# Attention queries of a two-layer hybrid encoder: evicted with 64 partitions at a time, or with 128 and copies to their places

## Chip, cores and metric

The kernel runs on one NeuronCore of one Trainium2 chip. The metric is device time in microseconds (us), the median over runs of the same program; lower is better. The profile comes from one execution taken by the hardware profiler.

## What is computed

One inference step of a small encoder trunk with two layers for 1024 prompt frames and 32 sample frames (1056 columns in all), model width 1024, all in fp32. Layer 0 is an mLSTM mixer and a SwiGLU feed-forward; layer 1 is windowed attention with 16 query heads on 2 shared key/value heads of width 64, and a second feed-forward. Each sub-layer ends in `x = LayerNorm(alpha * x + sublayer(x))`. The part that matters here:

```python
q = (x @ w_q).reshape(B, nc, CHUNK, N_KV_HEADS, GROUP, HEAD_DIM)
s = einsum('bcqhgd,bckhd->bchgqk', q, k) * (HEAD_DIM ** -0.5) + bias
mx = maximum(max(s, -1), sink)
p = exp(s - mx)
p = p / (sum(p, -1) + exp(sink - mx))
o = einsum('bchgqk,bckhd->bcqhgd', p, v)
```

Frames see their own chunk of 64 and the two chunks before it, with an ALiBi bias and a learned sink per head.

## The kernel before

**Precision.** Each fp32 operand of a large product is split into a rounded high part and a low part (the rest), both of type fp32r. `gemm` (L352) makes each product from three matmuls: high times high (L360), high times low (L361), low times high (L362). ScalarE rounds the high part and VectorE or GpSimd subtracts it to get the low part; for weights this is `Weights._next` (L182, the cast at L200 and the subtraction at L202). Raw weights come in by DMAs on SyncE's queue (`load_to`, L159) into three buffers, and a load is issued as soon as the second half of the unit three before it has been split, so it waits for the subtraction that read that buffer.

**Order.** Instructions are emitted in program order, engine by engine, and each engine and SyncE's queue run them in that order. `Weave` (L69) interleaves tasks: after each step of a `gemm` (three matmuls) it advances a clock by an estimate of the step's time, and every task (a generator) whose pause is over emits its next piece. So a task's `yield 2.0` means "go on after 2.0 us of projection have been emitted". Where the program must wait for a task without a projection to emit, it ticks the clock by 0.25 with nothing in between.

**Attention** (layer 1). The 1056 columns lie in three groups g of 384, 384 and 288 (`GRP`). Pairs of query heads are numbered j = 0 to 7. `q_group(j, g)` (L1574) projects one pair for one column group (8 steps of `gemm`) into a PSUM bank `d`, and makes the tile `Q` of shape [128, 2, 384]: for the first head of the pair (index 0) the high part on partitions 0 to 63 and the low part on 64 to 127; for the second head (index 1) the high part on 64 to 127 and the low part on 0 to 63. The key tiles `KH` and `KL` carry the keys twice along the partitions, so one matmul over 128 partitions multiplies high and low parts of a query at once. Before the change ScalarE writes the two high parts (L1580, L1581), 64 partitions each, and VectorE the two low parts (L1582, L1585), across to the other half of the partitions. There are four buffers of `Q`, so a group is projected only after the scores of the group four before it are emitted (L1785).

The queries come in the order `QG` (L1758): the four (j, 0) of j = 0 to 3 are projected first (L1627), then keys and values of the other columns, then the remaining 20 groups while attention runs. `attention` (L1650) is a pipeline over blocks (j, b) of 128 queries, three blocks to a group: `scores` (four matmuls L1669, L1670 into the two banks `psS`, which VectorE empties with bias and row minimum, L1675), `soft` (exponentials on ScalarE, L1687; reciprocal on VectorE, L1691; scaling on GpSimd, L1693), `turn` (transposes by TensorE into the one bank `T`, L1713; high part by ScalarE, L1716; low part by VectorE, L1717), `values` (L1728, L1729) and `place` (L1737, L1739). The scores of a group are emitted only when `ast["ready"]` says that its queries are made; the task `q_made` (L1777) raises it 2.0 us of emitted projection after the group's projection.

SyncE's queue carries, besides the weights, the copies that spread the keys over both partition halves (`k_spread`, L1547 to L1551, 96 KB each for a group of 384 columns), the bias tiles (L1607, L1608), and late in attention the reloads of the residual (L1098, L1100). `mixed_parts` (with L390 and L391) splits the attention output for the next projection while attention still runs.

Of the kernel before, what the change touches and what calls it, by code (L numbers as in the profile page):

```python
# [9 lines left out]
F32 = mybir.dt.float32  # L10
F32R = mybir.dt.float32r
AF = mybir.ActivationFunctionType
ALU = mybir.AluOpType
# [3 lines left out]
P = 128  # L17
# [223 lines left out]
def kernel(ctx: ExitStack, tc: tile.TileContext, A, O):  # L241
    nc = tc.nc
    ctx.enter_context(tc.manual_schedule())
    wv = Weave()
# [3 lines left out]
    def pool(name, space=None, side=None):  # L248
        kw = {}
        if space is not None:  # L250
            kw["space"] = space
        if side is not None:
            kw["side"] = side
        return tc.tile_pool(name=name, bufs=1, reuse_waits="tile", **kw)

    def new(p, tag, shape, dt=F32, bufs=1):
        uid[0] += 1
        return p.tile(list(shape), dt, name=f"{tag}_{uid[0]}", tag=tag, bufs=bufs)
# [124 lines left out]
    def project(u, g):  # L383

        ps = psdense(g)
        gemm(ps, wcols(u), xcols(g))
        return ps
# [1138 lines left out]
    pb = eb.enter_context(pool("pb"))  # L1526
# [47 lines left out]
    def q_group(j, g):  # L1574

        t0, n = GRP[g]
        ps = project(U_QB[g > 0][j], g)
        q = Q[j, g] = new(pb, "Q", [P, 2, 384], F32R, bufs=4)
        sc = -(HD ** -0.5)
        nc.scalar.activation(q[0:64, 0, :n], ps[0:64], AF.Copy, scale=sc)  # L1580
        nc.scalar.activation(q[64:128, 1, :n], ps[64:128], AF.Copy, scale=sc)  # L1581
        nc.vector.scalar_tensor_tensor(  # L1582
            q[64:128, 0, :n], ps[0:64], sc, q[0:64, 0, :n].bitcast(F32), op0=ALU.mult, op1=ALU.subtract
        )
        nc.vector.scalar_tensor_tensor(  # L1585
            q[0:64, 1, :n], ps[64:128], sc, q[64:128, 1, :n].bitcast(F32), op0=ALU.mult, op1=ALU.subtract
        )

    ck = new(pb, "ck", [P, P])
    nc.sync.dma_start(ck[:], A["cache_k"])  # L1590
# [4 lines left out]
    def v_parts(c, src, L):  # L1595

        src = src.rearrange("p (g d) -> p g d", g=2)
        nc.scalar.copy(VR[:L, c, :, 0, :], src)
        nc.vector.tensor_sub(VR[:L, c, :, 1, :], src, VR[:L, c, :, 0, :].bitcast(F32))
# [25 lines left out]
        wv.drain(t)  # L1625
    keys_values(0)
    for j in range(4):  # L1627
        q_group(j, 0)
        W.done(U_QB[0][j])
    for t in tasks[2:]:  # L1630
        wv.drain(t)
# [7 lines left out]
    def v_turn(group, pause):  # L1639
        yield pause  # L1640
        for c, c0, L, g, off in CH:
            if g == group:
                pt = new(psb, "O", [P, 512], bufs=2)
                nc.tensor.transpose(pt[:L, :P], vT[g][:, off : off + L], ident[:])
                v_parts(c, pt[:L, :P], L)
                ast["v"] = c + 1
                yield 0.8
# [112 lines left out]
    visits = [*range(4), *range(8)]  # L1760
    for t in spread:
        wv.drain(t)
    wv.launch(v_turn(0, 0))
    task = wv.launch(attention((GAP_A,) * 8))
    ast["ready"] = 4
# [9 lines left out]
    nc.sync.dma_start(O["s_v"], vT[2][:, 256:])  # L1775

    def q_made():  # L1777
        yield 2.0
        ast["ready"] += 1

    for i, (j, g) in enumerate(QG):
        if i < 4:
            continue

        while ast["scored"] < 3 * (i - 3):  # L1785
            wv.tick(0.25)
        q_group(j, g)
        wv.launch(q_made())
        if g == 2:
            W.done(U_QB[1][j])  # L1790
        if (j, g) == (7, 0):
            nparts[0] = 0
            parts = wv.launch(
                mixed_parts(
                    scr,
                    lambda g: ast["ready"] > QG.index((7, g)),
                    lambda k, g: ast["placed"] >= 3 * QG.index((k, g)) + 3,
                    (1.6, 1.0, 1.0),
                )
            )  # L1800
# [145 lines left out]
```

## Time and profile before

| | |
|---|---|
| median of 3 runs | 2269.16 us (2268.02 to 2269.37) |
| the profiled execution | 2261.86 us, span 2259.8 us, mean granted TensorE clock 0.996 |
| first and last query eviction in the span | 1212.2 us and 1413.6 us |
| ScalarE query instructions (L1580, L1581) | 24 each, median 480 and 486 ns |
| VectorE query instructions (L1582, L1585) | 24 each, median 550 and 559 ns |
| SyncE's queue (q1) | 284.38 MB, 37.1% of the DMA engines' time |
| DMA, mean over the span | 129 GB/s |

How to read it: times in the profile are us from the start of the span, durations of single instructions are ns or us as marked. PE is TensorE's matmul, PEld its weight load, DVE is VectorE, ACT ScalarE, POOL GpSimd, SP SyncE. A group of rows names the line, engine, operation, `out<-in`, shapes (partitions x elements) and count. "idle before, releaser" is the time that an engine stood still ahead of an instruction and what ended it.

### The profile page before, as it was taken

The page shows a single profiled execution, that of the slowest core. Times are in us where ns is not written, and L with a number is a line of the kernel's source. Part 1 is how long each engine was busy: PE and PEld are TensorE (multiplying, and loading weights), DVE is VectorE, ACT ScalarE, POOL GpSimd, SP SyncE. Part 2 cuts the span into 40 slices and gives each one's busy share as a digit, 9 for nine tenths or more (in the row PEclk, how much of TensorE's full clock was granted, in tenths as well). Part 3 has the DMA queues.
Part 4 walks back from the last instruction along what each step waited for, and adds up shares of the span by engine and source line. Part 5 has one row for each costly group of instructions (what it writes and reads, how often), then busy time and mean ns, then how long its engine had stood idle before and what let it go on. Part 6 is the DMA issues. An engine that isn't in the chain of part 4 may idle for free. (4 is left out here: it accounts for less than half of the span.)

```text
span 2259.8 us, 44187 instructions
## 1 busy us (share of the span) xinstructions
PE 2189.0 (97%) x17086; PEld 2149.0 (95%) x17086; DVE 1490.3 (66%) x2807; ACT 1015.3 (45%) x2285; POOL 1135.6 (50%) x1042
## 2 busy tenths in 40 slices
PE   9999999998999999999998999999999999999997
PEld 9899999998999999999997998899899999999997
DVE  4465577778666665566667778877666666466657
ACT  4443354455444444322246778756444444421124
POOL 2544333226666666544326776633666666554422
PEclk9999999999999999999999999999999999999999
DMA  4222112211434443697424211421343344397712
GB/s 148 74 54 69 53 39 85 96 39 66 150 137 153 158 143 139 219 333 234 162 79 138 85 60 44 137 72 47 115 152 140 135 146 163 124 334 259 248 57 77
DMA packets 167393, 291.52 MB, mean 129 GB/s; under 512 B 16592, under 2 KB 123144, under 8 KB 167184
## 3 DMA queue, kind: packets, MB, share of 16 engines
q1 hardware_dynamic: 162832, 284.38, 37.1%
q10 hardware_dynamic: 4352, 4.33, 0.5%
q8 instruction: 134, 2.20, 0.4%
q14 instruction: 75, 0.61, 0.1%
HBM read 203.89 MB, written 82.94 MB: 127 GB/s over the span
## 5 line engine op out<-in xcount | busy, mean ns | idle before, releaser
L202 POOL TENSOR_TENSOR wl_s<-wr,wh_s 128x512 fp32r<-128x512 f32 x224 | 316.8, 1435 | 241.3 <-ACT wh_s L200 158.2
L360 PE MATMUL d<-sx,wh 128*128 128x264 f32 (+2 forms) x1068 | 340.2, 319 | 1.2 <-DVE act L1505 0.7
L362 PE MATMUL d<-sx,wl 128*128 128x264 f32 (+2 forms) x1068 | 325.6, 305 | 8.4 <-DVE wl L202 6.0
L361 PE MATMUL d<-sx,wh 128*128 128x264 f32 (+2 forms) x1068 | 324.6, 304 | 3.8 <-DVE sx L474 2.6
L200 ACT CAST wh_s<-wr 128x512 fp32r<-128x512 f32 x224 | 135.5, 617 | 316.6 <-DVE wr L177 289.2
L360 PE MATMUL A<-sx,wh_s 128*128 128x264 f32 x896 | 254.6, 284 | 3.3 <-ACT z L1338 3.3
L202 POOL TENSOR_TENSOR wl<-wr,wh 128x512 fp32r<-128x512 f32 (+2 forms) x103 | 141.4, 1379 | 231.7 <-ACT wh L200 200.6
L361 PE MATMUL A<-sx,wh_s 128*128 128x264 f32 x896 | 254.2, 284 | 0.0
L362 PE MATMUL A<-sx,wl_s 128*128 128x264 f32 x896 | 254.0, 283 | 0.0
L362 PEld LDWEIGHTS d<-sx,wl 128*128 128x128 f32 x1068 | 200.9, 188 | 10.8 <-DVE wl L202 7.6
L361 PEld LDWEIGHTS d<-sx,wh 128*128 128x128 f32 x1068 | 201.6, 189 | 5.8 <-DVE sx L474 3.1
L360 PEld LDWEIGHTS d<-sx,wh 128*128 128x128 f32 x1068 | 201.7, 189 | 5.1 <-ACT z L443 1.1
L202 POOL TENSOR_TENSOR wl_a<-wr,wh_a 128x512 fp32r<-128x512 f32 x112 | 169.4, 1520 | 49.0 <-ACT wh_a L200 42.2
L362 PE MATMUL d<-sx,ex 128*128 128x264 f32 x624 | 178.5, 286 | 5.0 <-DVE ex L202 4.9
L360 PE MATMUL d<-sx,ex 128*128 128x264 f32 x624 | 181.0, 290 | 0.8 <-ACT sx L390 0.8
L361 PE MATMUL d<-sx,ex 128*128 128x264 f32 x624 | 178.2, 286 | 1.8 <-DVE sx L391 1.7
L360 PEld LDWEIGHTS A<-sx,wh_s 128*128 128x128 f32 x896 | 168.4, 188 | 3.7 <-ACT z L1338 3.7
L362 PEld LDWEIGHTS A<-sx,wl_s 128*128 128x128 f32 x896 | 168.9, 188 | 0.0
L361 PEld LDWEIGHTS A<-sx,wh_s 128*128 128x128 f32 x896 | 168.4, 188 | 0.0
L1208 POOL TENSOR_TENSOR z<-z 128x528 fp32r<-128x528 f32 x76 | 105.2, 1384 | 105.0 <-issue 53.2
L1693 POOL TENSOR_SCALAR s<-s,st 128x256 f32<-128x256 f32 (+1 forms) x144 | 124.2, 874 | 55.7 <-DVE st L1691 46.4
L1207 ACT CAST z<-z 128x528 fp32r<-128x528 f32 x136 | 85.8, 631 | 97.8 <-DVE z L1220 47.7
(334 smaller groups left out, 7404.2 us busy)
## 6 DMA issues: line engine op xcount, KB each, us to landing
wr<-in_gu SPq DMA_DIRECT2D x96, 512.0 KB, 4.5
hs_x<-z SPq DMA_DIRECT2D x72, 528.0 KB, 2.8
hs_t<-z SPq DMA_DIRECT2D x64, 528.0 KB, 4.1
sx<-hs_x SPq DMA_DIRECT2D x112, 264.0 KB, 6.0
sx<-hs_t SPq DMA_DIRECT2D x64, 264.0 KB, 6.0
ex<-hs_t SPq DMA_DIRECT2D x64, 264.0 KB, 6.2
wr<-in_dn SPq DMA_DIRECT2D x32, 512.0 KB, 5.2
ex<-hs_x SPq DMA_DIRECT2D x32, 264.0 KB, 6.1
```

Of the source, the lines that this page charges most:

```text
L200: self.nc.scalar.copy(hi, r)
L202: eng.tensor_sub(lo, r, hi.bitcast(F32))
L360: nc.tensor.matmul(out, ah, bh, start=start and k == 0, stop=False, **kw)
L361: nc.tensor.matmul(out, ah, bl, start=False, stop=False, **kw)
L362: nc.tensor.matmul(out, al, bh, start=False, stop=stop and k == last, **kw)
L1207: nc.scalar.copy(hi.bitcast(F32R), buf(s))
L1208: eng.tensor_sub(lo.bitcast(F32R), buf(s), hi)
L1693: nc.gpsimd.tensor_scalar_mul(p[:R, h, lo:256], p[:R, h, lo:256], st[:R, 2, h : h + 1])
```

## The change

`q_group` now writes the high parts of both heads with one ScalarE instruction of 128 partitions into a tile `qh`, and the low parts with one VectorE instruction of 128 partitions into a tile `ql` (two buffers each, 128 x 384). A task `place`, launched by `q_group`, waits for 1.0 us of emitted projection and then issues four DMAs on SyncE's queue that copy 64 partitions each to the four places in `Q`. The task that raises `ast["ready"]` waits for 4.0 us in place of 2.0. Ahead of the start of attention the last of the first four placements is emitted at the latest. The matmuls are the same in number and shape; their order in attention follows from the tasks.

```diff
@@ q_group
         q = Q[j, g] = new(pb, "Q", [P, 2, 384], F32R, bufs=4)
+        h, l = (new(pb, tag, [P, 384], F32R, bufs=2)[:, :n] for tag in ("qh", "ql"))
         sc = -(HD ** -0.5)
-        nc.scalar.activation(q[0:64, 0, :n], ps[0:64], AF.Copy, scale=sc)
-        nc.scalar.activation(q[64:128, 1, :n], ps[64:128], AF.Copy, scale=sc)
-        nc.vector.scalar_tensor_tensor(
-            q[64:128, 0, :n], ps[0:64], sc, q[0:64, 0, :n].bitcast(F32), op0=ALU.mult, op1=ALU.subtract
-        )
-        nc.vector.scalar_tensor_tensor(
-            q[0:64, 1, :n], ps[64:128], sc, q[64:128, 1, :n].bitcast(F32), op0=ALU.mult, op1=ALU.subtract
-        )
+        nc.scalar.activation(h, ps, AF.Copy, scale=sc)
+        nc.vector.scalar_tensor_tensor(l, ps, sc, h.bitcast(F32), op0=ALU.mult, op1=ALU.subtract)
+
+        def place():
+            yield 1.0
+            for i in range(2):
+                own, other = slice(64 * i, 64 * i + 64), slice(64 - 64 * i, 128 - 64 * i)
+                nc.sync.dma_start(q[own, i, :n].bitcast(F32), h[own].bitcast(F32))
+                nc.sync.dma_start(q[other, i, :n].bitcast(F32), l[own].bitcast(F32))
+
+        return wv.launch(place())
@@ the first four groups
-        q_group(j, 0)
+        placing = q_group(j, 0)
@@ ahead of attention
     for t in spread:
         wv.drain(t)
+    wv.drain(placing)
     wv.launch(v_turn(0, 0))
@@ q_made
-        yield 2.0
+        yield 4.0
         ast["ready"] += 1
```

## The prediction

> **What bounds the kernel now.** I read the page's engine shares first, then a table by stage of the stretch in which queries are made and used, then the waits of TensorE there, then single rows in order of time.
>
> ```profile
> span 2259.8 us, 44187 instructions
> ...
> PE 2189.0 (97%) x17086; PEld 2149.0 (95%) x17086; DVE 1490.3 (66%) x2807; ACT 1015.3 (45%) x2285; POOL 1135.6 (50%) x1042
> ```
>
> TensorE is busy for 97% of the span, so an edit to ScalarE and VectorE work pays only where TensorE waits for it. The stages (columns: stretch, length, then busy us of PE, PEld, DVE, ACT, POOL, then granted clock, DMA share, GB/s):
>
> ```profile
> 1210.00:1240.00 30.00, 22.24 (x125) 20.91 (x125) 22.89 (x50) 21.77 (x54) 20.72 (x19) 0.89 0.50 159
> 1240.00:1300.00 60.00, 58.27 (x429) 56.43 (x429) 46.38 (x174) 45.24 (x140) 43.82 (x57) 1.00 0.28 80
> 1300.00:1370.00 70.00, 69.59 (x507) 66.77 (x506) 56.65 (x215) 56.30 (x174) 51.73 (x65) 1.00 0.15 49
> 1370.00:1420.00 50.00, 44.38 (x329) 41.73 (x328) 45.01 (x155) 42.24 (x127) 30.48 (x36) 1.00 0.26 76
> ```
>
> The reader is to see two places with TensorE idle: 7.8 us in 1210 to 1240, where attention begins, and 5.6 us in 1370 to 1420, where VectorE is busy 90% and ScalarE 84%. From 1300 to 1370 TensorE has 0.4 us idle, and cheaper evictions buy nothing there. The waits of TensorE in 1200 to 1450 (total, times, longest):
>
> ```profile
> PE psS L1669 <- DVE st L1675: 6.6, 2, 5.6
> PE T L1713 <- DVE lo L1717: 5.2, 4, 2.3
> ```
>
> One wait of 5.6 us for VectorE to empty the score banks, and four for VectorE to empty the bank of the transposed probabilities. These are what can shrink.
>
> **The change part by part.** *Evictions.* 24 query groups each take two ScalarE and two VectorE instructions of 64 partitions:
>
> ```profile
> L1580 ACT ACTIVATE Q<-d x24: 386/480/488, 1212.2 to 1413.6; 64x384 fp32r<-64x384 f32 x16, 64x288 fp32r<-64x288 f32 x8
> L1581 ACT ACTIVATE Q<-d x24: 406/486/488, 1212.7 to 1414.0; 64x384 fp32r<-64x384 f32 x16, 64x288 fp32r<-64x288 f32 x8
> L1582 DVE SCALAR_TENSOR_TENSOR Q<-d,Q x24: 450/550/552, 1215.2 to 1415.1; 64x384 fp32r<-64x384 f32 x16, 64x288 fp32r<-64x288 f32 x8
> L1585 DVE SCALAR_TENSOR_TENSOR Q<-d,Q x24: 459/559/561, 1215.7 to 1415.5; 64x384 fp32r<-64x384 f32 x16, 64x288 fp32r<-64x288 f32 x8
> L1572 DVE COPY act<-d x3: 447/547/550, 1210.8 to 1263.5; 128x384 f32<-128x384 f32 x2, 128x288 f32<-128x288 f32 x1
> ```
>
> The last row reads the same kind of bank with all 128 partitions in 0.55 us, the time of the 64-partition forms. So one instruction does the work of two: about 0.48 us of ScalarE and 0.56 us of VectorE go per group, 11.5 and 13.4 us in all. Which of this lies on the path is a question of the place.
>
> *First scores.* After its first four score products TensorE waits for this chain:
>
> ```profile
> 1229.33 0.48 ACT L1580 ACTIVATE Q<-d 64x384 fp32r<-64x384 f32 x1
> 1229.83 0.49 ACT L1581 ACTIVATE Q<-d 64x384 fp32r<-64x384 f32 x1
> ...
> 1230.34 0.55 DVE L1582 SCALAR_TENSOR_TENSOR Q<-d,Q 64x384 fp32r<-64x384 f32 x1 [0.56 <-ACT Q L1581]
> 1230.91 0.56 DVE L1585 SCALAR_TENSOR_TENSOR Q<-d,Q 64x384 fp32r<-64x384 f32 x1
> 1231.50 0.29 DVE L1599 TENSOR_TENSOR VR<-O,VR 128x128 fp32r<-128x128 f32 x1
> 1231.71 0.28 DVE L1675 CUSTOM_DVE_ANT_0 s<-psS,bt 128x129 f32<-128x129 f32 x1
> ...
> 1232.05 0.58 PE L1669 MATMUL psS<-KH,Q 128*128 128x256 f32 x1 [5.61 <-DVE st L1675]
> ```
>
> In this order one ScalarE instruction (0.49) and one VectorE instruction (0.56) leave the chain. The group before it loses the same pair, but there the engines also waited for others. I take -1.2 us, a little over the 1.05 of one group; the ends are 0 (the value split, L1599, then waits for something else) and -2.1 (both groups in full). The two stretches around this wait ran at half clock:
>
> ```profile
> 1228.40:1231.80 3.40, 0.00 (x0) 0.00 (x0) 2.80 (x5) 2.76 (x6) 3.40 (x3) 0.50 0.76 194
> 1231.80:1235.20 3.40, 3.15 (x13) 3.06 (x14) 1.54 (x10) 1.59 (x8) 3.02 (x6) 0.50 0.30 106
> ```
>
> The 3.15 us of products in the second row would take half at full clock, so up to 1.6 us hang on whether the shorter wait still trips the clock; an earlier restart into the same slow stretch costs up to 0.6 more. I take 0. The Trainium skill, TensorE: Matmul & The Clock Gate, section "Part 1: The HAM clock gate", says that the clock halves after an idle window of some 3.4 us in a free-running grid; by it a wait cut from 5.6 to 4.4 us would contain a whole window less often, and the sum would be lower by up to 1.6 us. The rows agree on the 3.4 us, but the drop came while only the stretch before, partly busy, was over, so I do not count on it.
>
> *The copies.* Four SyncE copies of 96 KB per group, 96 in all. The nearest rows are the copies of the keys, between partition halves with the same shape:
>
> ```profile
> L1548 SPq DMA_DIRECT2D KH<-KH x4: 594/596/605, 1205.8 to 1262.7; - x4
> ...
> DMA to landing us min/median/max: 2.2/2.2/2.2
> ...
> DMA to landing us min/median/max: 3.6/3.9/4.2
> ...
> DMA to landing us min/median/max: 2.0/2.0/2.0
> ```
>
> (The landings are of L1548, L1547 and L1551.) Four issues of 0.6 take 2.4 us of SyncE, and a copy lands 2.0 to 4.2 us after its issue: a query is whole some 4 to 6 us after its low part, less the 1 us that the shorter evictions give. Attention needs the first group after the restart soonest:
>
> ```profile
> 1269.26 0.36 SPq L159 DMA_DIRECT2D wr<-in_wqb  x1
> ...
> 1270.11 0.56 DVE L1585 SCALAR_TENSOR_TENSOR Q<-d,Q 64x384 fp32r<-64x384 f32 x1
> ...
> 1271.20 0.28 PE L1669 MATMUL psS<-KH,Q 128*128 128x256 f32 x1
> ```
>
> Scores come 0.5 us after the query is done, so unmoved they would stall by 3 to 4 us. The longer delay of q_made moves them: in the emitted order the scores of this group now stand five projection steps later (one of 288 and four of 384 columns, some 2.5 us). SyncE is free at 1269.7, issues until about 1272, and the last copy lands at 1273.4 to 1275.6; the moved scores are due at 1273.8. So 0 to 1.8 us, and I take 0.2, as the last copy of a run is like the 2.0 rows. Later groups have room; the last one is evicted at 1413.60 and scored 25 us later:
>
> ```profile
> 1413.60 0.40 ACT L1580 ACTIVATE Q<-d 64x288 fp32r<-64x288 f32 x1
> ...
> 1438.64 0.28 PE L1669 MATMUL psS<-KH,Q 128*128 128x256 f32 x1
> ```
>
> *Lost cover.* Projection is fixed in amount, and attention starts 2.5 us later beside it. What runs alone at the restart is missing later: in the emitted order the attention steps that follow each other without a projection step between go from 11 to 18. What one costs, from both ends:
>
> ```profile
> 1345.11 0.28 PE L1729 MATMUL O<-lo,VR 128*128 128x256 f32 x1
> 1345.22 0.28 PE L1669 MATMUL psS<-KH,Q 128*128 128x256 f32 x1
> ...
> 1407.75 0.63 PE L1713 MATMUL T<-ident,s 128*128 128x128 f32 x4 [2.34 <-DVE lo L1717]
> ```
>
> Values and next scores back to back at 1345 cost nothing (0.11 apart, the pace). Three such places in a row at 1404 cost 2.3 us. Of the new ones five are single, and one cluster of three lies near the 36th block. I take 1.5 us for all; the ends are 0 and 6 (0.9 each).
>
> *The late stage.* The 2.3 us wait itself hung on VectorE:
>
> ```profile
> 1404.62 0.45 DVE L1582 SCALAR_TENSOR_TENSOR Q<-d,Q 64x288 fp32r<-64x288 f32 x1
> 1405.09 0.46 DVE L1585 SCALAR_TENSOR_TENSOR Q<-d,Q 64x288 fp32r<-64x288 f32 x1
> ...
> 1406.91 0.69 DVE L1717 TENSOR_TENSOR lo<-T,hi 128x512 fp32r<-128x512 f32 x1
> ```
>
> Six groups are evicted from 1370 to 1420, so up to 3.4 us of VectorE time go in a stage with 5.6 us of idle TensorE. The order is the same there before and after. I take half, -1.7; the ends are 0 (waits for GpSimd and ScalarE step in) and -5.6 (all the idle time, if the 0.48 on ScalarE counts as well).
>
> **Sum**: -1.2 + 0 + 0.2 + 1.5 - 1.7 = -1.2 us. The profiled execution took 2261.86 us (span 2259.8 and 2.06 around it), so 2260.7 for one like it. The median of the runs shown is 2269.16, 7.3 above, so 2268.0.
>
> **The rivals.**
> *SyncE's order (slower).* The copies stand in one queue with the weight loads, and these wait for buffers:
>
> ```profile
> SPq L159 <- POOL wl L202: 94.3, 12, 19.9
> ```
>
> Twelve waits, 7.9 us in the mean. A query behind one lands 7.9 + 2.4 + 2.2 = 12.5 us after its low part. In the first three groups after the restart the room is 0.5 to 4 us now and some 3 to 7 after the move: one such case stalls TensorE by 6 to 9 us, and the sum becomes +5 to +8, 2275. It decides where a load in front of a query is issued over 3 us after the query's low part is made. For it: the second group after the restart stands behind such a load. Against: at 1269 the load went out before the query was done. Chance 0.27, with dearer lost cover counted in, which leads to the same side at 6 us without relief.
> *VectorE was the bound (faster).* If the late stage runs at the pace of VectorE and ScalarE, all of the 5.6 us go, and with the first scores -6.8, and up to 1.6 of the clock: 2261 to 2262.4. For it: 90% busy, and the longest wait there behind VectorE. Against: no wait there names a query eviction itself. Chance 0.28.
> *The change does not do what it says*: 128 partitions cost twice 64. Then nothing is relieved and the sum is +1.7, 2270.9. The L1572 row speaks against it; 0.02, inside the forecast's band.
> By the Trainium skill, DMA: Bandwidth & Descriptors, section "Rules for kernel authors", two transfers to disjoint partition halves serialise and one of 128 partitions is better; by it the last copy of four lands late, as in the 3.6 to 4.2 rows, which makes 1.8 of the 0.2 above and the sum +0.4.
>
> **How the numbers follow.** The forecast, within 0.2% (4.5 us, about what a measurement of this kernel can tell from no change), has 0.45 with the third rival; faster 0.28; slower 0.27. The range reaches from the fast rival's 2262 to the slow one's 2275.
>
> **What would show it.** Right: query evictions x24 on each engine at 0.48 and 0.55 us; the 5.6 us wait near 4.4; scores of the fifth group some 2.5 us later against its projection without a long wait; TensorE idle in 1370 to 1420 down by about 2 us. Wrong: a wait of scores or weights for a copy of several us, SyncE waiting with copies behind a load, half clock at a second place, or new waits of the transposes between 1300 and 1370 that add up to over 4 us.

## The result, and the profile after

The changed kernel takes 2263.38 us (median of 20 runs, 2258.93 to 2268.05), the kernel before, run beside it, 2267.94 us (20 runs, 2263.73 to 2272.42). The ratio is 0.9983, 95% interval 0.9977 to 0.9990: 2.3 to 5.2 us faster. That is inside the band of 0.2% that was forecast, at its fast edge, where the sum had said 1.2 us.

The two profiled executions must not be subtracted. That of before took 2261.86 us, 6 us under the median of its runs; that of after took 2266.14 us, 3 us over its own. The mean granted clocks say which way each was lucky (one row from the view of the cores for before, then for after):

```profile
core 0: 2259.8 us, clock 0.996
```

```profile
core 0: 2263.9 us, clock 0.992
```

What can be compared is each stage. From the page of after, the engine shares, against the row shown of before: VectorE is 15.7 us and ScalarE 11.5 us less busy.

```profile
PE 2197.0 (97%) x17086; PEld 2157.3 (95%) x17086; DVE 1474.6 (65%) x2783; ACT 1003.8 (44%) x2261; POOL 1136.1 (50%) x1042
```

The rows of the two eviction lines and of the copies in after (count, minimum/median/maximum in ns, first and last start):

```profile
L1581 ACT ACTIVATE qh<-d x24: 395/482/498, 1213.9 to 1414.4; 128x384 fp32r<-128x384 f32 x16, 128x288 fp32r<-128x288 f32 x8
```

```profile
L1582 DVE SCALAR_TENSOR_TENSOR ql<-d,qh x24: 445/547/559, 1216.8 to 1415.4; 128x384 fp32r<-128x384 f32 x16, 128x288 fp32r<-128x288 f32 x8
```

```profile
L1588 SPq DMA_DIRECT2D Q<-qh x48: 461/505/618, 1218.4 to 1418.1; - x48
...
DMA to landing us min/median/max: 2.0/2.3/4.7
```

Half as many instructions of the same length, and 96 copies (48 of this line, 48 of L1589) with an issue of about half a microsecond. The view could tell the landing of only a few of them. The table by stage of after (columns as before: stretch, length, busy us of PE, PEld, DVE, ACT, POOL, granted clock, DMA share, GB/s):

```profile
1210.00:1240.00 30.00, 24.83 (x136) 22.68 (x135) 20.23 (x44) 18.59 (x45) 22.36 (x22) 0.94 0.78 220
1240.00:1300.00 60.00, 56.58 (x402) 54.83 (x403) 39.91 (x154) 40.12 (x127) 39.32 (x51) 0.97 0.40 108
...
1370.00:1420.00 50.00, 47.08 (x358) 45.41 (x357) 42.93 (x162) 41.92 (x130) 34.77 (x43) 1.00 0.40 114
```

Against before, TensorE's busy time goes up by 2.6 us in the first row and 2.7 us in the last (1370 to 1420), and down by 1.7 us in the second. The waits of TensorE in after, 1200 to 1450 (total, times, longest):

```profile
PE psS L1673 <- DVE st L1679: 4.0, 2, 3.1
PE T L1717 <- DVE st L1695: 2.8, 3, 1.5
PE T L1717 <- DVE lo L1721: 2.6, 4, 1.0
PE psS L1673 <- DMA Q<-qh: 1.4, 1, 1.4
...
PE psS L1673 <- DMA Q<-ql: 0.3, 1, 0.3
```

The wait of the first scores fell from 5.6 to 3.1 us, those of the transposes for their low part from 5.2 to 2.6, while those for the reciprocal (`st`) rose from 2.1 to 2.8; and one new wait of 1.4 + 0.3 us stands for the copies at the restart. A fourth place is outside the stages that I had looked at: in 1450 to 1500, where attention runs out, after has a wait for a split of the next weights that before has not. The waits of TensorE there, before and then after:

```profile
PE d L362 <- DVE ex L202: 2.0, 1, 2.0
...
```

```profile
PE d L362 <- DVE ex L202: 2.2, 1, 2.2
...
PE d L362 <- POOL ex L202: 1.2, 1, 1.2
PE ln L421 <- DVE z L602: 0.4, 1, 0.4
```

**A ledger by matmul number.** All kernels here issue the same 17086 matmuls. So I lined up two profiles by the number of the matmul. A stretch at half clock (granted 0.50) slows the work that falls into it, whichever that is; so I took from each time half of TensorE's busy time in the stretches at half clock up to there, and read how many us each stage is longer than in the first profile of before (minus is faster). Stages by number, with their times in before: first scores 9100 to 9250 (1206 to 1241 us), restart 9450 to 9550 (1270 to 1284), middle 9550 to 10200 (to 1373), late stage 10200 to 10500 (to 1420), end of attention 10500 to 11000 (to 1488). "Half clock" is what was taken off over the whole span, in us.

| profile | first scores | restart | middle | late | end | half clock |
|---|---|---|---|---|---|---|
| before, second profile (e9) | -0.7 | 0.0 | 0.0 | 0.0 | -0.1 | 11.0 (first: 3.2) |
| after | -2.1 | +1.7 | -0.5 | -3.9 | +1.9 | 13.4 |
| e1 change without the delay | -1.7 | +6.3 | -1.1 | -3.9 | +0.5 | 9.9 |
| e2 delay alone | 0.0 | 0.0 | +2.6 | +1.1 | +1.7 | 14.9 |
| e3 relief alone | -3.6 | 0.0 | -1.1 | -3.9 | -0.4 | 11.8 |
| e4 first three groups direct | -2.8 | 0.0 | +0.2 | -4.2 | -0.2 | 8.5 |
| e5 change in the first four groups | -3.0 | 0.0 | 0.0 | 0.0 | +0.4 | 10.2 |
| e6 change in the last twelve | +1.0 | 0.0 | -0.2 | -4.1 | +0.3 | 15.8 |
| e7 relief, copies nobody reads | -1.1 | 0.0 | -1.0 | -3.9 | -0.4 | 9.4 |
| e8 change at both ends | -2.5 | 0.0 | 0.0 | -4.1 | -0.1 | 14.3 |
| e10 halves, no crossing | 0.0 | 0.0 | 0.0 | -0.4 | -0.7 | 11.5 |
| e11 first copies from ScalarE | -2.6 | +0.2 | -0.4 | -3.9 | +1.5 | 13.8 |
| e12 relief and delay | -3.7 | 0.0 | -0.5 | -3.7 | +1.3 | 9.5 |

How far to trust it: where nothing was altered, the first column reads between -0.7 (e9) and +1.0 (e6), and the kernels whose first four groups are evicted alike spread from -1.1 to -3.7 in it, so it is good to about 1.3 us. Restart and middle repeat to 0.2, the late stage to 0.4 and the end to 0.7 (e10). In the four kernels with the delay in every group the matmuls from 9459 to 10229 stand in another order, which counts up to 0.4 us of the middle's work to the restart. Ahead of 9100 and behind 11000, where no kernel differs, the ledger still moves by -1.4 to +2.0 and -2.6 to +0.6 us; so it tells stages, not totals.

### The profile page after: what moved, and what is told of

Same layout as the page of the kernel before. It is cut to its first block, busy times and chain, and to the rows that moved or that the text cites. A ratio compares the mean times of both kernels' runs of the same rounds, so it can differ in the third digit from the quotient of the medians.

```text
span 2263.9 us, 44340 instructions
## 1 busy us (share of the span) xinstructions
PE 2197.0 (97%) x17086; PEld 2157.3 (95%) x17086; DVE 1474.6 (65%) x2783; ACT 1003.8 (44%) x2261; POOL 1136.1 (50%) x1042
## 4 chain that ended last, share of the span: by engine, by line
PE 79%; DVE 8%; ACT 4%; DMA 3%; issue 3%; POOL 2%; SPq 1%; ACTq 0%; DVEq 0%; POOLq 0%
PE A L360 9%; PE A L362 9%; PE A L361 9%; PE d L360 9%; PE d L362 9%; PE d L361 8%; PE B L360 7%; PE B L361 7%; PE B L362 7%; PE T L1717 1%; DMA wr<-in_dn 1%; PE T L904 1%; DMA hs_t<-z 1%; PE psS L1673 1%; PE H L900 1%
## 5 line engine op out<-in xcount | busy, mean ns | idle before, releaser
L361 PEld LDWEIGHTS d<-sx,wh 128*128 128x128 f32 x1068 | 204.3, 191 | 5.7 <-DVE sx L474 3.0
L360 PEld LDWEIGHTS d<-sx,wh 128*128 128x128 f32 x1068 | 204.3, 191 | 4.9 <-ACT z L443 1.1
L360 PE MATMUL A<-ex,wh_s 128*128 128x264 f32 x448 | 127.7, 285 | 1.3 <-ACT z L1321 1.3
```

The lines of the kernel that those rows point to most:

```text
L360: nc.tensor.matmul(out, ah, bh, start=start and k == 0, stop=False, **kw)
L361: nc.tensor.matmul(out, ah, bl, start=False, stop=False, **kw)
```

## The experiments

Two theories stood after the result. **Mine**: halving the evictions gains in two stages, and the copies' wait, the delay of q_made and the lost cover take part of it back. **The rival**: the order of the copies on SyncE (or the new order of the matmuls) does it, and the evictions matter little. Each was measured beside the kernel before on the same chip, whose medians were 2269.13 (e1 to e4), 2267.64 (e5 to e8) and 2267.28 us (e9 to e12).

### e1: the change without the longer delay

```diff
     def q_made():
-        yield 4.0
+        yield 2.0
```

> The change with q_made back at 2.0: copies as in the change, matmul order as before it. Theory A (cheaper evictions gain 6 to 7 us at two places, the first scores and the late stage; the restart at the fifth group gives back about 2): the scores of the fifth group stand where they stood before, 0.5 us behind the low part, and wait some 4 us for the copies in place of 1.7, so 2 to 3 us slower than the change, 2.5 us faster than before (ratio 0.9989). Theory B (the missing cover of the later start is what the change pays): 11 bare places in place of 18, so 1 to 3 us faster than the change (ratio 0.997).

Measured: 2271.07 us, ratio 1.0003 (0.9994 to 1.0011). The matmuls stand in the order of before. The waits of TensorE in e1, 1200 to 1450:

```profile
PE psS L1673 <- DMA Q<-qh: 3.8, 1, 3.8
PE psS L1673 <- DVE st L1679: 3.7, 3, 2.8
...
PE psS L1673 <- DMA Q<-ql: 2.2, 2, 1.6
```

The scores at the restart now wait 3.8 and 2.2 us for copies, where my theory had some 4, and the whole gain is gone, where it had 2.5 us left. So the path through the DMA does cost some 6 us at this one place, and the delay buys 4.6 of them back. The late stage keeps its gain (-3.9), with the order of before.

### e2: the delay alone, with the evictions of before

```diff
     def q_made():
-        yield 2.0
+        yield 4.0
```

> The kernel before with q_made at 4.0 and nothing else: old evictions, the matmul order of the change. Theory A: bare places cost little, 0 to 2 us slower than before (ratio 1.000 to 1.001). Theory B: 4 to 6 us slower (ratio 1.002 to 1.0026), in new waits of the transposes between 1300 and 1370 us.

Measured: 2278.29 us, ratio 1.0044 (1.0031 to 1.0057): slower by 7 to 13 us, more than I had allowed for. The waits of TensorE in e2, 1300 to 1450, then two of its stretches at half clock, each with the 3.4 us ahead of it (columns as in the table by stage):

```profile
PE T L1713 <- DVE st L1691: 6.9, 8, 2.3
PE T L1713 <- DVE lo L1717: 2.8, 3, 2.4
```

```profile
1386.30:1389.70 3.40, 1.53 (x11) 1.40 (x11) 3.28 (x13) 2.67 (x9) 2.21 (x3) 0.99 0.22 60
1389.70:1393.10 3.40, 3.40 (x16) 3.30 (x15) 1.89 (x9) 1.22 (x5) 2.31 (x3) 0.50 0.26 65
1413.60:1417.00 3.40, 1.07 (x9) 0.87 (x9) 3.28 (x12) 2.71 (x9) 1.42 (x3) 0.99 0.22 77
1417.00:1420.40 3.40, 3.40 (x17) 3.40 (x16) 2.17 (x6) 2.71 (x8) 3.40 (x4) 0.50 0.29 119
```

Here is the lost cover at its full price. With the old evictions TensorE waits eight times for the reciprocal (2.1 us in all before, 6.9 now), and after such waits it runs 3.4 us at half clock while it is fully busy, which before did in neither of its profiles between 1300 and 1450. The ledger has 5.2 us of waits. The clock pays the rest: its mean over the eleven runs is 0.9899, against 0.9922 over the 28 of before, and 0.0023 of 2278 us is 5.2 us more. The two make some 10 us together, against 9.2 between the medians.

### e3: the relief alone

The pair of 128-partition instructions writes straight into `Q`, the highs to its first index and the lows to its second; no copies, and the delay of 2.0.

```diff
+        h, l = q[:, 0, :n], q[:, 1, :n]
         sc = -(HD ** -0.5)
...
+        nc.scalar.activation(h, ps, AF.Copy, scale=sc)
+        nc.vector.scalar_tensor_tensor(l, ps, sc, h.bitcast(F32), op0=ALU.mult, op1=ALU.subtract)
```

> One ScalarE and one VectorE instruction of 128 partitions write straight into Q, no copies, q_made at 2.0, the matmul order of before. The low part of the first head and the high part of the second stand in the wrong places, so the scores are not the reference's; the amount of work is that of the change without its copies. Theory A: 6 to 7 us faster than before (ratio 0.997), about 2 us faster than the change. Theory C (the gain of the change is not the evictions): within 2 us of before.

Measured: 2258.72 us (5 runs), ratio 0.9957 (0.9945 to 0.9969), 7 to 12 us faster. Both stages gain (-3.6 and -3.9) and nothing is given back. This is more than twice the change's 4.6, so the copies and the delay together cost about as much as they leave. My theory had expected only 6 to 7 us.

### e4: the first three groups after the restart direct

The change, but the groups that attention needs soonest keep the four instructions of before and the delay of 2.0.

```diff
+    DIRECT = ((0, 1), (0, 2), (1, 1))
...
+        if (j, g) in DIRECT:
...
+            return None
...
+        wv.launch(q_made(2.0 if (j, g) in DIRECT else 4.0))
```

> The change, but the fifth to seventh group (the first three after the restart) are evicted as before, straight into Q, and are ready after 2.0; all others by copies and 4.0. Matmul order nearly that of before. Theory A: no wait of scores for copies, the reliefs stay: 6 to 7 us faster than before, 1.5 to 2 us faster than the change. Theory B gives the same sign with 11 bare places; it differs from A in e2. Theory C: like the change.

Measured: 2263.97 us, ratio 0.9980 (0.9970 to 0.9989). The wait at the restart and the wait at the end are gone (0.0 and -0.2 in the ledger), yet the time is not under the change's, where my theory had put it 1.5 to 2 us lower.

### e5, e6 and e8: the change in some groups only

The same switch with other lists: e5 applies the change to the first four groups alone, e6 to the last twelve alone, e8 to the first four and the last eight. The list shown is that of e8, against e4.

```diff
-    DIRECT = ((0, 1), (0, 2), (1, 1))
+    DIRECT = ((0, 1), (0, 2), (1, 1), (1, 2), (2, 1), (2, 2), (3, 1), (3, 2), (4, 0), (4, 1), (4, 2), (5, 0))
```

> Only the first four groups (ahead of attention) are evicted by the change's pair of instructions and its copies, the other 20 as before; matmul order exactly that of before. Theory A (the gain is the evictions at the first scores and in the late stage): 2 to 3.5 us faster than before, all of it between 1210 and 1240 us, the late stage unchanged at some 5.6 us idle. Theory D (the copies themselves cost time by their traffic or by holding up the weight loads): 0 to 2 us faster.

> Only the last twelve groups by the pair and copies, the first twelve as before; matmul order exactly that of before. Theory A: the wait of 5.6 us at the first scores stays, the late stage gains about 4 us; 3 to 5 us faster than before. Theory D: 0 to 2 us faster, the late stage's gain given back in waits for weights.

> The first four and the last eight groups by the pair and copies, the twelve between as before; matmul order exactly that of before, no scores near a copy. Theory A: both gains, no restart loss: 5 to 7 us faster than before, faster than the change by 1 to 2. Theory D: 2 to 4 us faster, no better than the change.

Measured: e5 2266.49 us, ratio 0.9991 (0.9983 to 1.0000); e6 2265.63 us, 0.9989 (0.9981 to 0.9997); e8 2263.21 us, 0.9980 (0.9971 to 0.9989). The order of the matmuls is that of before in all three. The stage 1370 to 1420 of e5, then of e6:

```profile
1370.00:1420.00 50.00, 44.34 (x330) 41.76 (x330) 45.16 (x154) 41.67 (x126) 30.55 (x36) 1.00 0.25 71
```

```profile
1370.00:1420.00 50.00, 48.17 (x362) 46.17 (x360) 44.19 (x164) 41.74 (x129) 35.34 (x43) 1.00 0.35 93
```

e5 leaves the late stage as it was (44.34 us of TensorE busy, 44.38 before), e6 lifts it to 48.17. So each stage's gain comes from the evictions in that stage; in the ledger the gains add (e8), and the order of the matmuls has no part in them. The times say less: the medians are 1.2, 2.0 and 4.4 us under before, each below what theory A had expected (2 to 3.5, 3 to 5, 5 to 7) and, but for e8's by 0.4, within theory D, by which the copies themselves cost time. The profiles speak for A, and e7 tests D by itself.

### e7: the relief, with the copies into a tile that nobody reads

```diff
+        d = new(pb, "qd", [P, 2, 384], bufs=2)
...
-                nc.sync.dma_start(q[own, i, :n].bitcast(F32), h[own].bitcast(F32))
-                nc.sync.dma_start(q[other, i, :n].bitcast(F32), l[own].bitcast(F32))
+                nc.sync.dma_start(d[own, i, :n], h[own].bitcast(F32))
+                nc.sync.dma_start(d[other, i, :n], l[own].bitcast(F32))
```

> e3_relief_alone with all 96 copies issued as in the change, but into a tile that nothing reads: the pair of instructions writes straight into Q (the low part of the first head and the high part of the second in the wrong places), no scores wait for a copy. Matmul order that of before. Theory A (copies cost only where scores wait for them): like e3_relief_alone, 8 to 10 us faster than before. Theory D (the copies cost by being issued): 4 to 6 us faster, like the change and e4_first_three_direct.

Measured: 2259.91 us (5 runs), ratio 0.9963 (0.9951 to 0.9975), as e3 within the intervals, whose middles lie 1.4 us apart. 96 issues on SyncE, their traffic and their place among the weight loads cost nothing that can be measured here. What costs is that somebody waits for them.

### e9: the kernel before, a second profile

No edit.

> The kernel before, unaltered, for a second profile of it. All theories expect 0 +- 0.1% against before. What it tells apart: the first profile of before (2261.9 us) lies 6 us under the median of its runs, with a mean granted clock of 0.996 against 0.992 in the runs. If that profile was short because it had few stretches at half clock, this one has more of them and a span near 2265 us, while the waits of the attention read as before: 5.6 us ahead of the first scores and 5.6 us of idle TensorE between 1420 and 1450 us, each within 0.5 us. If those waits differ by more than 1 us, the stage gains that I read from one pair of profiles (about 2 to 3 us at the first scores, about 4 us in the late stage) are partly noise.

Measured: 2268.47 us, ratio 1.0000 (0.9991 to 1.0009). The waits of TensorE, 1200 to 1450:

```profile
PE psS L1669 <- DVE st L1675: 6.6, 2, 5.6
PE T L1713 <- DVE lo L1717: 4.7, 3, 2.3
PE T L1713 <- DVE st L1691: 2.1, 5, 0.7
```

The same waits as in the first profile, to 0.5 us, and a span of 2267.5 us, 7.7 us longer. The stretches at half clock took 11.0 us here and 3.2 us there: 7.8 us, the whole difference. So the baseline's stages were read rightly, and only its total was lucky. (The idle time that the expectation places at 1420 to 1450 is that of 1370 to 1420; the ledger's late column, 0.0, compares it.)

### e10: four half-partition instructions that do not cross

```diff
-        nc.scalar.activation(q[64:128, 1, :n], ps[64:128], AF.Copy, scale=sc)
+        nc.scalar.activation(q[64:128, 0, :n], ps[64:128], AF.Copy, scale=sc)
...
-            q[64:128, 0, :n], ps[0:64], sc, q[0:64, 0, :n].bitcast(F32), op0=ALU.mult, op1=ALU.subtract
+            q[0:64, 1, :n], ps[0:64], sc, q[0:64, 0, :n].bitcast(F32), op0=ALU.mult, op1=ALU.subtract
...
```

> Four instructions of 64 partitions per group as before, two on ScalarE and two on VectorE, but each writes to the partitions that it reads from: highs into the first index of Q, lows into the second. So the scores are of other numbers than the reference's (the two queries of a pair are mixed up); their count, shapes and order are those of before. Theory (the gain of the relief is half as many instructions): the same as before, within 2 us, 0 to -2. Rival (what is dear before is the crossing of partition halves, or other data in Q raise the granted clock): -4 us or more, 2263 or less, with the half-partition instructions shorter than 0.48 and 0.55 us or a clock above 0.993.

Measured: 2267.76 us, ratio 1.0000 (0.9991 to 1.0009). The VectorE row of e10, beside 450/550/552 before:

```profile
L1582 DVE SCALAR_TENSOR_TENSOR Q<-d,Q x24: 445/549/551, 1214.4 to 1416.5; 64x384 fp32r<-64x384 f32 x16, 64x288 fp32r<-64x288 f32 x8
```

Crossing the partition halves costs nothing that shows, and the data of e3 and e7 do not make them faster by themselves. The gain is the halved number of instructions.

### e11: the copies of the restart from ScalarE's queue

```diff
+                eng = nc.scalar if (j, g) in ((0, 1), (0, 2)) else nc.sync
-                nc.sync.dma_start(q[own, i, :n].bitcast(F32), h[own].bitcast(F32))
-                nc.sync.dma_start(q[other, i, :n].bitcast(F32), l[own].bitcast(F32))
+                eng.dma_start(q[own, i, :n].bitcast(F32), h[own].bitcast(F32))
+                eng.dma_start(q[other, i, :n].bitcast(F32), l[own].bitcast(F32))
```

> The change, with the copies of the two restart groups issued from ScalarE's DMA queue, where no weight load stands ahead of them, rather than SyncE's. Theory (the copies' way to Q costs 1.7 us at the restart, 1.4 and 0.3 us of TensorE's waits, of which part is SyncE issuing four copies one behind another behind a weight load): 1 to 2 us faster than the change, 0.9975 of before, about 2262. Rival (the wait is given back: the projection steps that cover it are merely late, and ScalarE now pays four issues of about 0.5 us while evictions wait): the same as the change within 1 us, 2263 to 2264.

Measured: 2263.10 us, ratio 0.9985 (0.9975 to 0.9994), no faster than the change. Rows of the restart in order of time, first of after, then of e11:

```profile
1269.60 0.56 DVE L1582 SCALAR_TENSOR_TENSOR ql<-d,qh 128x384 fp32r<-128x384 f32 x1 [0.45 <-ACT qh L1581]
1270.49 0.38 SPq L159 DMA_DIRECT2D wr<-in_wqb  x1
1270.96 0.47 SPq L1588 DMA_DIRECT2D Q<-qh  x1
...
1272.78 0.60 SPq L1589 DMA_DIRECT2D Q<-ql  x1
...
1275.82 0.36 PE L1673 MATMUL psS<-KH,Q 128*128 128x256 f32 x1 [1.38 <-DMA Q<-qh]
...
1276.55 0.35 PE L1673 MATMUL psS<-KH,Q 128*128 128x256 f32 x1 [0.26 <-DMA Q<-ql]
```

```profile
1271.17 0.56 DVE L1582 SCALAR_TENSOR_TENSOR ql<-d,qh 128x384 fp32r<-128x384 f32 x1 [0.45 <-ACT qh L1581]
1271.23 0.51 ACTq L1589 DMA_DIRECT2D Q<-qh  x1
...
1273.10 0.61 ACTq L1590 DMA_DIRECT2D Q<-ql  x1
...
1275.85 0.28 PE L1674 MATMUL psS<-KH,Q 128*128 128x256 f32 x1
...
1276.88 0.62 ACT L200 CAST wh<-wr 128x512 fp32r<-128x512 f32 x1 [2.03 <-DMA Q<-ql]
```

In after a weight load and the pause before the copies put 0.8 us between the end of the low part (1270.16) and the first issue, and the scores come 5.66 us after that end, 1.38 of them as a wait. In e11 the first copy goes out before the low part is done, and the scores come 4.12 us after its end without a wait. The stage did what my theory said; the time did not follow. ScalarE pays for it: between 1271.2 and 1276.8 eight issues of 0.5 to 0.6 us hold it for 4.5 us, and the weight split behind them starts at 1276.88. Whether this alone eats the 1.5 us, the runs don't settle; the intervals allow a gain on the change of up to about 2 us.

### e12: relief and delay, without the copies

e3 with `q_made` at 4.0, so the matmuls stand in the order of after.

```diff
     def q_made():
-        yield 2.0
+        yield 4.0
```

> The pair of 128-partition instructions writes straight into Q (highs into the first index, lows into the second, no copies, so the scores are of other numbers than the reference's), and the first scores may start only 4.0 instead of 2.0 after their evictions, so that the matmuls stand in the order of the change. Theory (the moved cover costs almost nothing once the evictions are halved): within 2 us of the same kernel with 2.0, that is -7 to -10 against before, 2258 to 2261; then what the change lacks of that is the copies' wait at the restart. Rival (the lost cover is what eats the gain): about the change's -4.5, 2263 to 2264.

Measured: 2261.73 us (8 runs), ratio 0.9973 (0.9963 to 0.9983). It lies between the two theories: 5.6 us under before, where e3 has 10.4, e7 7.7 and the change 4.6. The waits of TensorE in 1450 to 1500, first of e12, then of e3:

```profile
PE d L362 <- DVE ex L202: 2.2, 1, 2.2
PE d L362 <- POOL ex L202: 0.9, 1, 0.9
PE ln L421 <- DVE z L602: 0.3, 1, 0.3
```

```profile
PE d L362 <- DVE ex L202: 2.1, 1, 2.1
```

With cheap evictions the delay costs little in the middle and late stages (0.6 and 0.2 us against e3, where the dear ones had 2.6 and 1.1 against before); it costs 1.7 us at the end of attention (+1.3 against -0.4 in e3), where the next weights are split too late. This wait of 0.9 to 1.3 us for GpSimd's split stands in the profiles of all four kernels with the delay in every group (after, e2, e11, e12); of those without it, e5 has 0.9, e6 0.5 and e1 0.2, and the others none; so the delay is not its only cause.

## Why the prediction was right, and where its steps were off

The direction of the sum, the place in the 0.2% band and both named stages held. The sizes did not: by the ledger both gains were priced too low, by 0.9 and 2.2 us, and the restart too cheap by 1.5. That these partly cancel is luck: the misses of the gains alone would have put the sum at -4.3, next to the band's edge of 4.5. From 9100 to 11000 the ledger gives the change -3.0, where the steps had given -1.2 and the medians have -4.6 (-2.3 to -5.2).

- **Evictions: right.** 24 instructions each at 482 and 547 ns, as the L1572 row had said for VectorE; e10 shows that only their number matters.
- **First scores, -1.2: the term was too small.** The wait fell by 2.5 us, from 5.6 to 3.1; it is 2.8 to 3.2 us in all nine profiles with halved evictions of the first four groups and 5.3 to 5.6 in the other five. Rows of after in order of time: from the start of ScalarE's instruction to that of the value split L1603 it is 1.19 us, where before had 2.17 (L1580 to L1599). This 1.0 us is the one group that I had counted. Counted from matmul 9000, which starts at 1188.64 in before and at 1189.78 in after, ScalarE comes to this group after 40.7 us in before and 39.8 in after: 0.9 us more, as the group before lost its pair too. The last 0.6 us is no gain, for TensorE itself came to the wait that much later in this profile. So the stage gained 1.9 us, near the end that I had put at -2.1 for "both groups in full".

```profile
1229.59 0.48 ACT L1581 ACTIVATE qh<-d 128x384 fp32r<-128x384 f32 x1
...
1230.11 0.56 DVE L1582 SCALAR_TENSOR_TENSOR ql<-d,qh 128x384 fp32r<-128x384 f32 x1
...
1230.78 0.29 DVE L1603 TENSOR_TENSOR VR<-O,VR 128x128 fp32r<-128x128 f32 x1
...
1231.33 0.38 PE L1673 MATMUL psS<-KH,Q 128*128 128x256 f32 x1 [3.14 <-DVE st L1679]
```

- **Half clock, 0: near at the first scores, and missed at the restart.** The wait of 3.1 us still tripped the clock, here as in all nine profiles that have it. The rule of the Trainium skill that I had weighed (TensorE: Matmul & The Clock Gate, section "Part 1: The HAM clock gate"), by which a shorter wait contains a whole idle window less often, would have let the drop vanish; it did not. What became of it is smaller: in the five profiles with the old evictions two stretches in a row run at half clock there and take 1.6 to 3.1 us, of which the first profile of before has the least; in the nine with halved ones it is one stretch and 1.6 to 1.7 us (e11: two, 2.8). The traces show why the drop stays: a stretch of 3.4 us need not be idle, it can be enough that TensorE is busy for about half of it. After has two such pairs, here and at the restart, where TensorE is busy for only 1.77 of 3.40 us around the waits for the copies:

```profile
1229.10:1232.50 3.40, 1.17 (x8) 1.07 (x8) 2.55 (x9) 2.53 (x9) 3.40 (x3) 1.00 0.86 217
1232.50:1235.90 3.40, 3.28 (x13) 2.48 (x12) 1.70 (x10) 1.37 (x6) 3.40 (x7) 0.50 0.99 245
1273.50:1276.90 3.40, 1.77 (x11) 1.30 (x10) 0.43 (x2) 0.31 (x2) 2.61 (x4) 1.00 0.88 196
1276.90:1280.30 3.40, 3.40 (x17) 3.30 (x15) 1.38 (x7) 1.20 (x4) 1.83 (x2) 0.50 0.84 266
```

  The second pair is the "half clock at a second place" that the prediction named as a sign of being wrong. It costs up to 1.7 us beside the 1.7 us of the waits, and the ledger, which leaves the half clock out, does not count it. e1, with longer waits there, has two such stretches (from 1275.0 and 1285.3), e11, without the waits, has none.
- **Restart copies, +0.2: too small, inside its bounds.** 1.4 + 0.3 = 1.7 us, next to the upper end of 1.8. I had taken the last copy of four to land like the fast rows (2.0). By the semaphore updates in the trace all four landed slowly, 4.3, 4.2, 3.9 and 3.6 us after their issues, at 1275.3 to 1276.4. The trace points to the weight load that went out at 1270.49, half a microsecond ahead of them: it landed 4.4 us after its issue, at 1274.9, and the copies behind it. The rows of this load and of a copy at 1297.85 with no load under way:

```profile
wr<-in_wqb SPq DMA_DIRECT2D x1, 512.0 KB, 4.4
```

```profile
Q<-ql SPq DMA_DIRECT2D x1, 96.0 KB, 2.0
```

  Over all 96 copies of after, the 43 issued while a weight load was under way landed after 4.1 us in the median, the other 53 after 2.2. With 2.2 here the last copy would have landed at 1275.0, about when its scores were due, so by this estimate the load makes nearly all of the 1.7 us. The rule that the prediction quoted from the Trainium skill (DMA: Bandwidth & Descriptors, section "Rules for kernel authors"), that transfers to disjoint partition halves serialise, spoke for the slow end too, but by another cause than the one that shows here: the four copies of the next group but one (issued from 1284.02, no load under way) landed 2.1 to 2.2 us after their issues, each, so this profile does not show halves waiting for each other. That unmoved copies stall by 3 to 4 us was too low as well: e1 has 6.3.
- **Lost cover, +1.5: the size was near, the place wrong.** In the middle, to whose end the order of the matmuls differs, after is no slower than before (-0.5) and e12 0.6 slower than e3; e2 shows that they cost 2.6 us there, and clock besides, while the evictions are dear. The cost came at the end of attention, +1.9, at a wait that I had not looked for: GpSimd's split of the next weights.
- **Late stage, -1.7: the step that failed most.** I took half of the 3.4 us of VectorE time for fear that waits for other engines would step in. (Three of the six groups have 288 columns and 0.46 us, so it is 3.1.) The ledger has -3.9 in every kernel with halved evictions there (-3.7 to -4.2 in nine profiles), over what VectorE alone gives and under all of the 5.6. The instructions that go are 5.7 us on both engines together; the chain goes through ScalarE to VectorE, so part of each may count, which is argued and not shown. After has 2.9 us of idle TensorE left in 1370 to 1420, of 5.6.
- **The rivals.** "VectorE was the bound" was nearer the truth than its 0.28: its relief in the late stage was real, and e3 and e7, with nothing to pay for it, reach 7 to 12 us and 6 to 11 us. "SyncE's order" described what e1 shows, a kernel whose gain is lost to copies; the delay of 4.0 is what keeps the change out of it. It was right that a weight load ahead of the copies decides, but not how: ahead of the copies of the first three groups after the restart no load held the queue for more than 1.3 us, and the one at the restart slowed the copies' landing by 2 us. e7 shows no cost of the queue where nobody waits.

**Where the relief's gain went.** e3 and e7 are 10.4 and 7.7 us under before, the change 4.6. By the ledger 1.7 us are the copies' wait at the restart and some 2.3 us the delay's wait at the end (+1.9 against -0.4). Runs and ledger agree on the order of the three (e3, e12, the change), but the interval of e12 overlaps both others, so the split into two parts is argued from the profiles and not shown by the times. It stays open why e4, e8 and e11, which each avoid one or both waits in their profiles, measure 2263 to 2264 us like the change: the ledger gives them -5.4 to -6.9, at or inside the far ends of their intervals. Against the second profile of before (e9, itself at -0.8) these are -4.6 to -6.1, inside all three, so the gap is no larger than the runs' noise. None of the kernels whose scores read the copies beats the change by more than the runs can tell.

## What to carry to other kernels

An engine that is only 66% busy over the span can still be the bound in a stage where it is 90% busy with TensorE idle beside it; price an eviction there by the whole chain through both engines, not by one. A detour through DMA costs what the first consumer waits for it, not its issues: 96 copies that nobody waits for cost nothing that could be measured, one group that was waited for cost 6 us. Look at what is under way on the DMA engines when they go out: behind a weight load these copies took about twice as long to land. Moving the consumer later pays for the detour only if what it uncovers is cheap, so look at where the moved work now ends, too.

## What the runs showed of the hardware

- **Half clock makes the difference between two profiles of one kernel.** Those of before have the same waits and differ by 7.7 us of span, and 7.8 us is TensorE's time at half clock. It comes in stretches of 3.4 us (now and then two in a row), each of which costs up to 1.7 us.
- **A half-idle stretch trips the clock.** Within each profile the stretches at half clock lie on one grid of 3.41 us. In the 14 profiles, cut along their grids, a stretch at full clock with TensorE busy for under 45% of it was followed by half clock 38 times of 38, between 45 and 64% 45 times of 165, and over 64% not once in 8859. Where the grid lies against the waits differs from profile to profile, so the same waits trip it in one and not in another.
- **Small waits are dearer than they look.** e2 added 5.2 us of waits by the ledger and 9.2 us of time (2278.29 against 2269.13).
- **Partition halves are neither cheaper nor dearer.** ScalarE and VectorE take 0.48 and 0.55 us for 64 or for 128 partitions of 384 columns, VectorE whether the output crosses to the other half or not (0.550 and 0.549 us).
